# A hybrid decoder layer on one core: another order for the first loads, and the 16 meta rows' statistics on another engine

## The chip, the cores and the metric

The kernel runs on one core of a Trainium2 chip. The metric is the device time of one execution in microseconds. Five engines work side by side, each with its own instruction queue: TensorE (PE, with its weight loads shown as PEld), VectorE (DVE), ScalarE (ACT), GpSimd (POOL) and SyncE (SP), which here issues nearly all loads and stores.

## The reference

One decoder layer on 16 learned meta rows and 1024 rows of `x`, each 1024 wide, all in 32-bit floats. Everything begins with a normalisation of each row and one wide projection:

```python
def rmsnorm(x, g):
    xf = x.astype(jnp.float32)
    y = xf * lax.rsqrt(jnp.mean(xf * xf, axis=-1, keepdims=True) + EPS)
    return (y * g.astype(jnp.float32)).astype(x.dtype)

h = jnp.concatenate([meta, x], axis=1)          # 16 + 1024 rows
a = rmsnorm(h, ln_mix_pre[l])
proj = a @ w_in[l]                              # 1024 -> 3584 columns
dq, dk, dv, hq, hf, hi, hg = jnp.split(proj, SPLITS, axis=-1)
y_diff = diff_attention(dq, dk, dv, ...)        # 4 heads
y_hgrn = hgrn2(hq, hf, hi, hg, ...)             # 4 heads, a gated recurrence
mix = jnp.concatenate([y_diff, y_hgrn], axis=-1) @ w_out[l]
h = h + rmsnorm(mix, ln_mix_post[l])
a = rmsnorm(h, ln_ffn_pre[l])
y = conv_ffn(a, ...)                            # 1024 -> 5632, conv of 3, gelu, 2816 -> 1024
h = h + rmsnorm(y, ln_ffn_post[l])
return h[:, N_META:, :]
```

The change touches only the first `rmsnorm`, for the first 272 rows.

## The kernel before

The rows are cut into nine blocks: block 0 holds the 16 meta rows, blocks 1 to 8 hold 128 rows of `x` each. The projection takes them in three groups of three blocks, so the first matmuls of the first group need blocks 0, 1 and 2. To keep the precision of 32-bit floats, each operand is split into a rounded part (`ahi`, `wh`) and the rest (`alo`, `wl`), and three products are summed.

For each block the first normalisation has these steps. `load_x` (L266) issues the load on SP, the meta rows' if the block is 0. `pre_stat` (L270) squares the rows on ScalarE with a running sum; then `rstd_of` (L169) turns the sum into the reciprocal root with two small ScalarE instructions, Ln and Exp. `pre_scale` (L278) multiplies one half (512 columns) by the root and by the gain, on VectorE. `pre_turn` (L283) transposes four squares of 128 columns on TensorE into one bank of its accumulator memory. `pre_hi` (L291) casts that into `ahi` on ScalarE, and `pre_lo` (L294) writes the rest into `alo` on VectorE.

The gain is one row of 1024 numbers, loaded into `grow` (L793). Two matmuls (L835) with a row of ones spread it over 128 partitions, 512 columns each, and VectorE copies each half into `gb`, which every `pre_scale` reads.

```python
def pre_stat(i):
    r = rows(i)
    xss[i] = zp.tile([P, D], F32, tag="xs", name=f"xs{i}", bufs=3)
    ss = zp.tile([P, 1], F32, tag="ss", name=f"ss{i}", bufs=3)
    A.activation(xss[i][:r], xts[i][:r], AF.Square, accum_out=ss[:r])
    rstd_of(ss[:r], ss[:r], D)
    return ss

def pre_scale(i, half, ss):
    r = rows(i)
    cs = slice(512 * half, 512 * half + 512)
    V.scalar_tensor_tensor(xss[i][:r, cs], xts[i][:r, cs], ss[:r], gb[:r, cs], ALU.mult, ALU.mult)
```

`weights(j, c)` (L821) splits half `c` of the weights of projection `j` (0 is `dq`, 1 is `dk`): the cast of `dq`'s weights is on ScalarE, that of `dk`'s on GpSimd, and the rest of both (`wl`) on GpSimd. The third, `dv`, follows later (`third_hi`, `third_lo`). Blocks 4 and 5 are scaled by `far_block` (L874): ScalarE multiplies by the root, GpSimd by the gain.

Order: TensorE runs in the order of the program throughout. From L828 (`state["ordered"] = True`) to L952 VectorE, ScalarE and GpSimd do so too; `V`, `A` and `G` are wrappers whose instructions all appear under L58 in the profile. After L952 a planner places the instructions of the engines other than TensorE by its own estimated times. SP issues the loads in the order in which they stand, each when its slot is free. `xt` tiles have three slots, which `grow`, block 0 and block 1 take first, and later blocks 6, 7 and 8; blocks 2 to 5 use spare memory (`X_in`). The transposes use a pool of five banks; the gain's two halves take two of them first, and the turned half (2, 1) takes the bank of (0, 0) again, so it waits for `pre_lo` of (0, 0).

Of the kernel before, what the change touches and what calls it, by code (L numbers as in the profile page):

```python
# [9 lines left out]
F32 = mybir.dt.float32  # L10
# [3 lines left out]
ALU = mybir.AluOpType  # L14
AX = mybir.AxisListType
PSUM = bass.MemoryType.PSUM

P = 128
# [3 lines left out]
D = 1024  # L22
# [19 lines left out]
def rows(i):  # L42
    return META if i == 0 else P
# [47 lines left out]
def layer_kernel(ctx: ExitStack, tc: tile.TileContext, x, meta, table, lbl, gpre, gpost, win,  # L91
# [3 lines left out]
    V, A = Ordered(tc, nc.vector, state), Ordered(tc, nc.scalar, state)  # L95
# [3 lines left out]
    def pool(name, bufs, side="left", space=None):  # L99
        kw = {"side": side} if space is None else {"space": space}  # L100
        cm = tc.tile_pool(name=name, bufs=bufs, reuse_waits="tile", **kw)
        return cm, cm.__enter__()
# [44 lines left out]
    def ps_m(name):  # L147
        return pp.tile([P, 512], F32, tag="m", name=name, bufs=deep["m"])
# [20 lines left out]
    def rstd_of(dst, ss, n):  # L169
        A.activation(dst, ss, AF.Ln, bias=eps[: dst.shape[0]], scale=1.0 / n)  # L170
        return A.activation(dst, dst, AF.Exp, scale=-0.5)
# [5 lines left out]
    def mix_tile(tag, dt, name):  # L177
        return mxp.tile([P, MIX[tag]], dt, tag=tag, name=name)
# [51 lines left out]
    z_cm, zp = pool("pre", 2, "right")  # L230
# [30 lines left out]
    xts, xss = {}, {}  # L261

    def spare_tile(tag):
        return mix_tile(tag, F32, f"{tag}_in")

    def load_x(i, where=None):  # L266
        xts[i] = zp.tile([P, D], F32, tag="xt", name=f"xt{i}", bufs=3) if where is None else where
        SY.dma_start(xts[i][: rows(i)], meta if i == 0 else x[P * (i - 1): P * i, :])
# [14 lines that stand above are left out]
    def pre_turn(i, half, pt):  # L283
        r = rows(i)
        for j in range(4):
            k = 4 * half + j
            T.transpose(pt[:, j * r:(j + 1) * r], xss[i][:r, P * k: P * (k + 1)], ident[:r, :r])
        pv = pt[:, : 4 * r].rearrange("p (k t) -> p k t", k=4)
        return pv, slice(4 * half, 4 * half + 4), slice(place(start(i)), place(start(i)) + r)

    def pre_hi(pv, ks, s):  # L291
        return A.copy(ahi[:, ks, s], pv)
# [325 lines left out]
    def attn_in(h):  # L618
        qs = [ap_.tile([P, L], F32R, tag=f"q{m}", name=f"q{m}_{h}") for m in range(2)]
        ks = [ap_.tile([P, L], F32R, tag=f"k{m}", name=f"k{m}_{h}") for m in range(2)]  # L620
        vn = ap_.tile([P, NBLK, P], F32, tag="avn", name=f"avn{h}")
        G.memset(vn[:, 0], 0.0)
        rr = ap_.tile([P, 256], F32, tag="rr", name=f"rr{h}")
        own = [slice(0, 64), slice(64, 128)]
        oth = [slice(64, 128), slice(0, 64)]

        def ev_q(g, b0, b1, t0, t1, pt):
            for m in range(2):
                A.mul(qs[m][own[m], t0:t1], pt[own[m]], 0.125)
            for m in range(2):  # L630
                V.scalar_tensor_tensor(qs[m][oth[m], t0:t1], pt[own[m]], 0.125, qs[m][own[m], t0:t1].bitcast(F32), ALU.mult, ALU.subtract)

        def ev_k(g, b0, b1, t0, t1, pt):
            for m in range(2):
                A.copy(ks[m][own[m], t0:t1], pt[own[m]])
            for m in range(2):
                V.tensor_tensor(kl[m][own[m], t0:t1], pt[own[m]], ks[m][own[m], t0:t1].bitcast(F32), op=ALU.subtract)
            for m in range(2):
                A.copy(ks[m][oth[m], t0:t1], ks[m][own[m], t0:t1].bitcast(F32))

        def ev_v(g, b0, b1, t0, t1, pt):
            vt = ap_.tile([P, 384], F32, tag="vt", name=f"vt{h}_{g}", bufs=1)
            A.copy(vt[:, : t1 - t0], pt)
            late.append((vn, vt, b0, b1, f"va{h}_{g}"))

        return (qs, ks, vn, rr), [(h, f"dq{h}", ev_q), (4 + h, f"dk{h}", ev_k), (8 + h, f"dv{h}", ev_v)]
# [144 lines left out]

    t_a, tiles = attn_in(0)
    grow = zp.tile([P, D], F32, tag="xt", name="grow", bufs=3)[:1]  # L793
    SY.dma_start(grow, gpre)
    spare = {n: spare_tile(t) for n, t in ((2, "X0"), (0, "X1"), (1, "X2"))}
    load_x(0)
    load_x(1)
    load_x(2, spare[2][:, :D])

    def raw_tile(j, c):  # L800
# [20 lines left out]
    def weights(j, c):  # L821
        hi = wp.tile([P, 512], F32R, tag="wh", name=f"wh_{tiles[j][1]}_{c}", bufs=4)
        lo = wp.tile([P, 512], F32R, tag="wl", name=f"wl_{tiles[j][1]}_{c}", bufs=4)
        (G.tensor_copy if j else A.copy)(hi, raws[j, c])
        G.tensor_tensor(lo, raws[j, c], hi.bitcast(F32), op=ALU.subtract)
        parts[j][c] = hi, lo

    state["ordered"] = True  # L828
    stat = {}
    for i in range(3):  # L830
        stat[i] = pre_stat(i)
    for half in range(2):
        cs = slice(512 * half, 512 * half + 512)
        pt = ps_m(f"pg{half}")
        T.matmul(pt, ones, grow[:, cs], start=True, stop=True)  # L835
        V.tensor_copy(gb[:, cs], pt)
        if half == 0:
            pre_scale(0, 0, stat[0])
    load_x(6)
    banks0 = {}  # L840
    for i in range(3):
# [1 line left out]
    turned = {}  # L843

    def turn(i, half):
        turned[i, half] = pre_turn(i, half, banks0[i][half])

    for i in (1, 2):
        for half in range(2):
            pre_scale(i, half, stat[i])  # L850
    pre_scale(0, 1, stat[0])
    for i, half in ((0, 0), (1, 0), (1, 1), (2, 0), (2, 1), (0, 1)):
        turn(i, half)
    pre_hi(*turned[0, 0])
    pre_hi(*turned[1, 0])
    weights(0, 0)
    pre_hi(*turned[2, 0])
    for i in range(3):
# [900 lines left out]
```

## Time and profile before

| | |
|---|---|
| three runs | 1276.09, 1278.28, 1279.64 us, median 1278.28 |
| the profiled execution | 1277.19 us, its span 1275.4 us |
| TensorE busy | 1256.7 us, 99% of the span |
| VectorE, ScalarE, GpSimd busy | 913.9, 687.3, 507.2 us |
| granted TensorE clock | 0.999 |

A row of the timeline has the start and the duration in microseconds, the engine, the line, the operation, what is written and read, and in brackets how long the engine had been idle before and what released it. `x4` behind a row means that neighbouring like instructions were merged. In a table by stretches, each row has the stretch, its length, the busy time of PE, PEld, DVE, ACT and POOL, the granted clock, the busy share of the DMA engines and the GB/s that they moved.

### The profile page before, as it was taken

What the parts mean: (1) busy time and instruction counts of PE and PEld (TensorE: products, weight loads), DVE (VectorE), ACT (ScalarE), POOL (GpSimd) and SP (SyncE); (2) the same over time, 40 slices, a digit from 0 to 9 for tenths busy, and PEclk for the clock granted to TensorE, in tenths of its full rate; (3) what the DMA queues carried; (4) which work ended last, traced back from release to release, by engine and by line L of the source; (5) the groups of instructions that cost most, each with busy time, mean ns of one, the idle gap of its engine ahead of it and who ended that gap; (6) DMA issues with size and microseconds to landing.
All of it is one profiled execution on the core that took longest, in us unless ns stands there. A gap on an engine that the chain in (4) does not pass through costs nothing.

```text
span 1275.4 us, 26064 instructions
## 1 busy us (share of the span) xinstructions
PE 1256.7 (99%) x10166; PEld 1172.8 (92%) x10166; DVE 913.9 (72%) x1492; ACT 687.3 (54%) x1638; POOL 507.2 (40%) x390
## 2 busy tenths in 40 slices
PE   8999999999999999999999999999999999999997
PEld 6999999999999998778899999999999998878886
DVE  7565646565656564457899888898898877797586
ACT  8475456546654754356764544445535445564554
POOL 5232423241323311353067676676776731020121
PEclk9999999999999999999999999999999999999999
DMA  7336555373734533787322221322222247955363
GB/s 260 96 60 131 89 139 94 83 146 92 132 94 79 125 82 113 232 279 253 131 67 67 92 88 63 100 76 75 92 75 83 75 116 258 351 184 173 91 215 124
DMA packets 116705, 165.04 MB, mean 129 GB/s; under 512 B 10131, under 2 KB 57811, under 8 KB 116582
## 3 DMA queue, kind: packets, MB, share of 16 engines
q1 hardware_dynamic: 93350, 151.84, 37.1%
q0 software_dynamic: 23232, 11.54, 7.7%
q8 instruction: 80, 1.31, 0.4%
q14 instruction: 43, 0.35, 0.1%
HBM read 134.24 MB, written 52.17 MB: 146 GB/s over the span
## 4 chain that ended last, share of the span: by engine, by line
PE 46%; DVE 4%; ACT 2%; issue 1%; POOL 1%; DMA 0%; SPq 0%; DVEq 0%; ACTq 0%; POOLq 0%
PE pd L1586 5%; PE pd L1587 5%; PE pd L1585 5%; PE pb L1412 4%; PE pb L1411 4%; PE pb L1413 4%; PE pc L1412 3%; PE pc L1411 3%; PE pc L1413 3%; PE pa L1412 3%; PE pa L1411 3%; PE pa L1413 3%; DVE xh L58 1%; DVE t L58 1%; DVE c L58 1%
## 5 line engine op out<-in xcount | busy, mean ns | idle before, releaser
L1412 PE MATMUL pb<-t,uh 128*128 128x258 f32 x504 | 141.0, 280 | 0.8 <-DVE t L58 0.8
L1411 PE MATMUL pb<-t,uh 128*128 128x258 f32 x504 | 140.5, 279 | 0.8 <-DVE u L58 0.8
L1413 PE MATMUL pb<-t,ul 128*128 128x258 f32 x504 | 140.2, 278 | 0.0
L1586 PE MATMUL pd<-wl,gh 128*128 128x512 f32 (+1 forms) x312 | 121.0, 388 | 1.1 <-DVE wl L58 1.1
L1585 PE MATMUL pd<-wh,gh 128*128 128x512 f32 (+1 forms) x312 | 120.8, 387 | 0.5 <-DVE x L58 0.5
L1587 PE MATMUL pd<-wh,gl 128*128 128x512 f32 (+1 forms) x312 | 120.7, 387 | 0.0
L58 DVE SCALAR_TENSOR_TENSOR c<-uu,cwt,c 128x514 f32<-128x514 f32 (+1 forms) x88 | 106.9, 1214 | 0.0
L58 DVE SCALAR_TENSOR_TENSOR c<-ug,cwt,c 128x514 f32<-128x514 f32 (+1 forms) x88 | 101.4, 1153 | 0.0
L1412 PEld LDWEIGHTS pb<-t,uh 128*128 128x128 f32 x504 | 94.8, 188 | 1.0 <-DVE t L58 1.0
L1411 PEld LDWEIGHTS pb<-t,uh 128*128 128x128 f32 x504 | 94.8, 188 | 1.0 <-DVE u L58 1.0
L58 ACT ACTIVATE c<-c 128x514 f32<-128x514 f32 (+1 forms) x44 | 27.9, 634 | 125.5 <-DVE c L58 125.5
L1413 PEld LDWEIGHTS pb<-t,ul 128*128 128x128 f32 x504 | 94.8, 188 | 0.0
L1412 PE MATMUL pc<-t,uh 128*128 128x258 f32 (+1 forms) x336 | 93.9, 279 | 0.0
L1412 PE MATMUL pa<-t,uh 128*128 128x258 f32 (+1 forms) x336 | 93.9, 279 | 0.0
L1411 PE MATMUL pa<-t,uh 128*128 128x258 f32 (+1 forms) x336 | 93.6, 278 | 0.0
L1411 PE MATMUL pc<-t,uh 128*128 128x258 f32 (+1 forms) x336 | 93.6, 278 | 0.0
L1413 PE MATMUL pc<-t,ul 128*128 128x258 f32 (+1 forms) x336 | 93.4, 278 | 0.0
L1413 PE MATMUL pa<-t,ul 128*128 128x258 f32 (+1 forms) x336 | 93.4, 278 | 0.0
L58 POOL TENSOR_TENSOR ul<-ws,uh 128x512 fp32r<-128x512 f32 x42 | 69.2, 1647 | 59.6 <-ACT uh L58 59.6
L58 POOL TENSOR_TENSOR ws<-ra,ra 128x512 f32<-128x512 f32 x42 | 67.9, 1617 | 60.9 <-DMA ra<-in_wup_dram 34.1
L58 POOL TENSOR_TENSOR c<-c,c 128x514 f32<-128x514 f32 (+1 forms) x44 | 68.8, 1564 | 53.9 <-ACT c L58 50.5
L58 DVE TENSOR_TENSOR ul<-ra,uh 128x512 fp32r<-128x512 f32 x43 | 41.5, 966 | 46.6 <-POOL ul L58 46.6
(389 smaller groups left out, 4183.1 us busy)
## 6 DMA issues: line engine op xcount, KB each, us to landing
ra<-in_wup_dram SPq DMA_DIRECT2D x88, 256.0 KB, 2.6
mp<-msc SPq DMA_DIRECT2D x23, 512.0 KB, 5.7
tsc<-in_wdown_dram SPq DMA_DIRECT2D x44, 256.0 KB, 5.2
wi<-tsc SPq DMA_DIRECT2D x44, 256.0 KB, 3.0
gi<-gsc SPq DMA_DIRECT2D x33, 256.0 KB, 4.2
wi<-in_wdown_dram SPq DMA_DIRECT2D x33, 256.0 KB, 5.2
gsc<-c SPq DMA_DIRECT2D x22, 257.0 KB, 2.1
tsc<-in_wdown_dram POOLq DMA_DIRECT2D x22, 256.0 KB, 7.2
```

What stands on the lines that cost most here:

```text
L58: ins = call(*args, **kw)
L1411: T.matmul(pt, hi[:, s], th[:, k], start=(first and k == 0), stop=False, skip_group_check=True)
L1412: T.matmul(pt, hi[:, s], tl[:, k], start=False, stop=False, skip_group_check=True)
L1413: T.matmul(pt, lo[:, s], th[:, k], start=False, stop=(k == 3), skip_group_check=True)
L1585: T.matmul(py, gh[:, s], wh, start=(k == 0 and pr not in (3, 7)), stop=False, skip_group_check=True)
L1586: T.matmul(py, gh[:, s], wl, start=False, stop=False, skip_group_check=True)
L1587: T.matmul(py, gl[:, s], wh, start=False, stop=(k == NH - 1), skip_group_check=True)
```

## The change

SP issues the load of block 1 first, then the meta rows, then `grow`; before it was `grow`, the meta rows, block 1. The meta rows' squares and their sum move from one ScalarE instruction to two VectorE instructions ahead of the gain's copies; the reciprocal root of the meta rows stays on ScalarE, now between the statistics of blocks 1 and 2. The first half of the meta rows is scaled behind both halves of block 1, where it was scaled between the gain's two copies. Its transposes go behind those of block 1, and its cast `pre_hi` behind that of (1, 0).

```diff
     t_a, tiles = attn_in(0)
     grow = zp.tile([P, D], F32, tag="xt", name="grow", bufs=3)[:1]
+    spare = {n: spare_tile(t) for n, t in ((2, "X0"), (0, "X1"), (1, "X2"))}
+    load_x(1)
+    load_x(0)
     SY.dma_start(grow, gpre)
-    spare = {n: spare_tile(t) for n, t in ((2, "X0"), (0, "X1"), (1, "X2"))}
-    load_x(0)
-    load_x(1)
     load_x(2, spare[2][:, :D])
...
     state["ordered"] = True
     stat = {}
-    for i in range(3):
-        stat[i] = pre_stat(i)
+    r = rows(0)
+    xss[0] = zp.tile([P, D], F32, tag="xs", name="xs0", bufs=3)
+    stat[0] = zp.tile([P, 1], F32, tag="ss", name="ss0", bufs=3)
+    V.tensor_tensor(xss[0][:r], xts[0][:r], xts[0][:r], op=ALU.mult)
+    V.reduce_sum(stat[0][:r], xss[0][:r], axis=AX.X)
+    stat[1] = pre_stat(1)
+    rstd_of(stat[0][:r], stat[0][:r], D)
+    stat[2] = pre_stat(2)
     for half in range(2):
         cs = slice(512 * half, 512 * half + 512)
         pt = ps_m(f"pg{half}")
         T.matmul(pt, ones, grow[:, cs], start=True, stop=True)
         V.tensor_copy(gb[:, cs], pt)
-        if half == 0:
-            pre_scale(0, 0, stat[0])
     load_x(6)
...
-    for i in (1, 2):
-        for half in range(2):
-            pre_scale(i, half, stat[i])
+    for half in range(2):
+        pre_scale(1, half, stat[1])
+    pre_scale(0, 0, stat[0])
+    for half in range(2):
+        pre_scale(2, half, stat[2])
     pre_scale(0, 1, stat[0])
-    for i, half in ((0, 0), (1, 0), (1, 1), (2, 0), (2, 1), (0, 1)):
+    for i, half in ((1, 0), (1, 1), (0, 0), (2, 0), (2, 1), (0, 1)):
         turn(i, half)
+    pre_hi(*turned[1, 0])
     pre_hi(*turned[0, 0])
-    pre_hi(*turned[1, 0])
     weights(0, 0)
     pre_hi(*turned[2, 0])
     for i in range(3):
         pre_lo(*turned[i, 0])
```

## The prediction

> **What bounds the kernel now.** I read the page first, then the busy time by stretches, because a change in the first microseconds is worth only what the stages behind it let through.
>
> ```profile
> span 1275.4 us, 26064 instructions
> PE 1256.7 (99%) x10166; PEld 1172.8 (92%) x10166; DVE 913.9 (72%) x1492; ACT 687.3 (54%) x1638; POOL 507.2 (40%) x390
> ```
> ```profile
> 0.00:26.00 26.00, 20.76 (x122) 16.73 (x123) 18.08 (x27) 21.15 (x46) 18.11 (x27) 1.00 0.79 282
> 26.00:60.00 34.00, 33.80 (x201) 31.07 (x200) 20.59 (x48) 18.85 (x45) 7.44 (x11) 1.00 0.34 105
> 60.00:200.00 140.00, 139.90 (x1355) 135.70 (x1356) 82.73 (x193) 83.59 (x250) 43.21 (x40) 1.00 0.52 108
> ...
> 400.00:600.00 200.00, 197.67 (x1583) 173.18 (x1582) 116.75 (x215) 109.65 (x325) 64.73 (x53) 1.00 0.57 169
> 600.00:800.00 200.00, 197.54 (x1630) 193.84 (x1629) 175.00 (x214) 111.12 (x215) 115.03 (x72) 1.00 0.28 91
> ```
>
> The second column of a stretch is its length, the third TensorE's busy time. TensorE is idle 5.2 us of the first 26 and only 0.3 of the next 174. So a delay or a gain that reaches TensorE's queue at 26 us goes through to the end; nothing behind it is slack that could swallow it. The question is what sets TensorE's pace in the first 26 us. I followed that through the timeline, engine by engine.
>
> ```profile
> 0.73 0.35 SPq L794 DMA_DIRECT2D grow<-in_gpre_dram  x1
> 1.14 0.33 SPq L268 DMA_DIRECT2D xt<-in_meta_dram  x1
> 1.52 0.41 SPq L268 DMA_DIRECT2D xt<-in_x_dram  x1
> 1.97 0.43 SPq L268 DMA_DIRECT2D X_in<-in_x_dram  x1
> ```
> ```profile
> 2.30 3.75 PE L835 MATMUL pg<-grow,ones 1*128 1x512 f32 x4 [2.30 <-DMA grow<-in_gpre_dram]
> 4.38 0.69 DVE L58 COPY gb<-pg 128x512 f32<-128x512 f32 x1 [4.38 <-PE pg L835]
> 6.08 0.69 DVE L58 COPY gb<-pg 128x512 f32<-128x512 f32 x1 [0.17 <-PE pg L835]
> 7.02 1.42 DVE L58 SCALAR_TENSOR_TENSOR xs<-xt,ss,gb 128x512 f32<-128x512 f32 x2 [0.24 <-ACT ss L58]
> ```
> ```profile
> 5.28 1.06 ACT L58 ACTIVATE xs<-xt 128x1024 f32<-128x1024 f32 x1 [0.37 <-DMA xt<-in_x_dram]
> 6.78 0.20 ACT L58 ACTIVATE ss<-ss 128x1 f32<-128x1 f32 x1
> 6.89 1.04 ACT L58 ACTIVATE xs<-X_in 128x1024 f32<-128x1024 f32 x1
> ```
>
> Columns are start, duration, engine, operation, and in brackets the idle time before it and its releaser. The scaling of block 1 (7.02) needs two things: the reciprocal root of block 1, ready at 6.78 + 0.20 = 6.98, and the gain row spread over the partitions, whose second half is copied by 6.08 + 0.69 = 6.77. The gain chain begins with the small load `grow`, and it is **only 0.2 us** ahead of the chain that the change wants to shorten. That is the centre of my argument.
>
> ```profile
> 7.83 3.18 PEld L287 LDWEIGHTS px<-ident,xs 128*128 128x128 f32 x16 [1.29 <-DVE xs L58]
> 6.06 0.58 PE L287 MATMUL px<-ident,xs 16*128 16x16 f32 x4
> 8.98 0.59 ACT L58 CAST ahi<-px 128x512 fp32r<-128x512 f32 x1 [0.29 <-PE px L287]
> 9.46 0.62 ACT L58 CAST wh_dq<-wr_dq 128x512 fp32r<-128x512 f32 x1
> 10.69 1.07 ACT L58 CAST ahi<-px 128x512 fp32r<-128x512 f32 x2 [0.60 <-PE px L287]
> 10.17 1.66 POOL L58 TENSOR_TENSOR wl_dq<-wr_dq,wh_dq 128x512 fp32r<-128x512 f32 x1 [6.17 <-ACT wh_dq L58]
> 14.96 1.07 POOL L58 CAST wh_dk<-X_in 128x512 fp32r<-128x512 f32 x1
> 21.27 2.53 POOL L58 TENSOR_TENSOR xs<-xs,gb 128x512 f32<-128x512 f32 x2 [0.88 <-ACT xs L58]
> 25.09 0.55 PEld L901 LDWEIGHTS pi_dv<-ahi,w 128*128 128x128 f32 x4 [0.81 <-POOL w L58]
> ```
>
> From 10.17 on GpSimd works with one gap of 0.88 us, and TensorE's last wait in the head, at 25.09, is for GpSimd. What starts GpSimd is the cast `wh_dq` on ScalarE at 9.46, queued there behind `pre_hi` of blocks 0 and 1. So the head's end is set by when that cast starts.
>
> **The change part by part.** Times are this trace's; the moved ones are worked out.
>
> *Block 1's load first.* It is issued at 0.73 in place of 1.52.
>
> ```profile
> xt<-in_x_dram SPq DMA_DIRECT2D x1, 512.0 KB, 3.7
> xt<-in_meta_dram SPq DMA_DIRECT2D x1, 64.0 KB, 2.0
> sub<-in_subln_dram SPq DMA_DIRECT2D x1, 0.5 KB, 7.8
> 4.00:4.50 0.50, 0.50 (x2) 0.33 (x1) 0.12 (x1) 0.40 (x3) 0.00 (x0) 1.00 0.96 393
> ```
>
> With the 3.7 us that it takes now (the last column: issue to landing) it lands at 4.43; its square and statistics take 5.28 to 6.98, that is 1.70, so its root is ready at 6.15, 0.8 earlier. The block of 512 KB after these three keeps its place.
>
> *`grow` third.* Issued at 0.73 + 0.45 + 0.38 = 1.56, the steps being those of the block and the meta rows now. When does it land? At the head of the queue it takes about 2.27 − 0.73 = 1.54 us; alone, it would land at 3.1. But `sub`, only 0.5 KB, takes 7.8 us when it is issued behind full blocks: a small load on this queue waits for the bytes ahead of it. By that row `grow` comes behind 512 and 64 KB, and the meta rows behind 512. At 393 GB/s (last column) 64 KB are 0.16 us, so meta and `grow` land at about 4.6. An upper end is 5.22, where the third load of the same 580 KB landed before (1.52 + 3.7). I take 4.6, nearest to the `sub` row, and keep 3.1 and 5.2 as ends. `grow` is **2.3 us later**.
>
> The Trainium skill, "DMA: Bandwidth & Descriptors", under "Queues, rings and completion order", says that each DMA engine takes the descriptors of one ring in order, which speaks against this move and agrees with the 7.8 us. Its fit under "Anatomy of one DMA" (about 2.0 us and the bytes over 436 GB/s, given for another queue kind) would have `grow` at 1.56 + 2.0 = 3.6 if nothing stood ahead; by that alone the end would come 1.0 us earlier than I forecast.
>
> *The gain chain.* From TensorE's start at 2.30 to the second copy at 6.08 it takes 3.78 us, so from 4.6 the second copy runs 8.4 to 9.1, and scaling of block 1 starts at 9.1 in place of 7.02: **+2.1**. The 0.8 that block 1 won ends in a wait.
>
> *Meta squares and sum on VectorE.* Two instructions on 16x1024, which the trace does not show; nearest are
>
> ```profile
> L58 DVE TENSOR_TENSOR t<-at,t 128x1024 fp32r<-128x1024 f32 x8 | 9.6, 1217 | 0.1
> L58 DVE TENSOR_REDUCE ast<-S 128x1 f32<-128x912 f32 x8 | 8.9, 1107 | 0.2
> 5.17 0.74 DVE L58 SCALAR_TENSOR_TENSOR xs<-xt,ss,gb 16x512 f32<-16x512 f32 x1
> ```
>
> The 16-row scaling of 512 costs as much as the 128-row one (0.74 against 1.42/2), so rows don't matter: 1.22 + 1.11 × 1024/912 = 2.5 us. From 4.6 that ends at 7.1. First gain copy 7.1 to 7.8, then a wait to 8.4: the work is hidden by TensorE's second gain matmul, with 0.6 to spare; if `grow` were early that cover would be gone, and the second copy would run 7.8 to 8.5. ScalarE sheds a 1.06 square but now waits from 6.15 to 7.1 in `rstd_of` for the sum, and block 2's square stands behind that: 7.6 in place of 6.89. Block 2's root then comes at about 9.3, needed only at 11. Free.
>
> *Order of scaling, turning and casts.* VectorE's scalings follow each other by about 0.7: (1,0) 9.1, (1,1) 9.8, (0,0) 10.4, (2,0) 11.1, (2,1) 11.8, (0,1) 12.5. TensorE turns four squares in about 0.85 (3.18 for sixteen loads, plus the drain), starting 0.8 after the scaling starts: (1,0) from 9.9, (1,1) 10.75, then (0,0) 11.6 to 12.2 (0.58 now). `pre_hi` of (0,0) has become the second cast and must wait for that: 12.3. Then `wh_dq` at 12.4 or 12.5 in place of 9.46. Of these 3.0 us, 2.1 are the gain chain and 0.9 the new place of (0,0), which now stands behind two turned halves of block 1 instead of ahead of them. This 0.9 has nothing to do with the load and stays even if `grow` is early.
>
> *Behind it.* GpSimd's chain starts 3.0 later and drags the `dk` weights, block 3's turn and the last wait at 25.09. ScalarE's own chain is 2.5 to 2.9 later (cast of (2,0) at about 13.3 in place of 10.69), so the gap of 0.88 may give back up to 0.3. I take **+2.9** at 26 us, and as ends +1.5 (0.6 + 0.9, if meta and `grow` both overtake) and +3.6 (`grow` at 5.2).
>
> *Slots.* `xt` has three slots, first held by `grow`, block 1 and the meta rows and then by blocks 6, 7 and 8. Block 8's load now waits for the meta rows' last scaling, at 13.2.
>
> ```profile
> xt<-in_x_dram SPq DMA_DIRECT2D x1, 512.0 KB, 8.5
> 29.40 1.05 ACT L58 ACTIVATE xs<-xt 128x1024 f32<-128x1024 f32 x1
> L58 ACT CAST wh_hf<-wr_hf x2: 620/621/622, 45.7 to 48.2; 128x512 fp32r<-128x512 f32 x2
> ```
>
> Even with 8.5 us it lands at 21.7 and is read at 29.4 or later; the small loads and the `hf` weights queued behind it on SP are used at 45.7. Nothing.
>
> **Sum.** The profiled execution took 1277.19 us, so + 2.9 is 1280.1 on its base; it lies 1.1 below the median of the runs, 1278.28. On the median the forecast is 1278.28 + 2.9 = **1281.2**. About 0.3% (3.8 us) is what a measurement can tell from no change, so this is a loss on the near side of that: over 1282.1 would be slower.
>
> **The rivals.** *The small loads overtake.* If meta (1.18 + 2.0 = 3.2) and `grow` (3.1) take only their own times, the sum ends at 5.7, the second gain copy at 7.6, scaling starts 0.6 late, and with the 0.9 the head loses 1.5: 1279.8. For it: the DMA engines still move little just then (66 GB/s, last column). Against it: the `sub` row.
>
> ```profile
> 2.50:3.00 0.50, 0.50 (x1) 0.26 (x2) 0.00 (x0) 0.00 (x0) 0.45 (x2) 1.00 0.58 66
> ```
>
> *A new order later gives it back (the other side).* From line 952 on, the instructions of all engines but TensorE are placed by a planner from its own due times, which the change shifts. Place: the stretches 400 to 800 us, where TensorE now idles 2.3 + 2.5 = 4.8 us. If all of that went, 1281.2 − 4.8 = 1276.4; it decides the sign once it gives back over 2.9. For it: only that these stalls exist. Against: everything behind 26 us shifts together, and then an order by due times stays.
>
> *A new order later costs a further stall.* The same mechanism the other way, one stall as large as one of these two stretches holds now: 1281.2 + 2.4 = 1283.6. A stage filled to 99.9% has more to lose than to win, so I hold it likelier than the gain.
>
> That the change does what it says, and block 1's turns start sooner, can't pay: even with `grow` where it was, the gain chain's 6.77 allows 0.2 us at (1,0), which the new place of (0,0) takes back.
>
> **How the numbers follow.** Forecast 0.48 (own range 1280.4 to 1282.3), overtaking 0.12, an order that gives back 0.08, an order that costs 0.32. The giving back lies 2 us above the border of 1274.4; half of its chance, and 0.01 for what I don't see, is faster: 0.05. Slower over 1282.1 is most of the costing order and the forecast's upper edge: 0.35. The rest, 0.60, is within 0.3%. The range runs from the giving order's upper part, 1278.6, over the overtaking case to 1284.5, a costing order with the head at its upper end.
>
> **What would show it.** In the changed profile: SP issues block 1, meta, `grow` at 0.7, 1.2 and 1.6; the gain matmul starts near 4.6 (near 3.1: overtaking); scaling of block 1 at 9.1 with its wait put to TensorE's `pg`, not to ScalarE's root; `wh_dq` at 12.4; GpSimd's first weight operation near 13.2; the `pi_dv` weight load of 25.09 near 28; TensorE's busy time in the first 26 us down by about 2.9. I am wrong if the gain matmul starts before 3 us, if `wh_dq` starts before 10.5, or if the stretches 400 to 800 us lose or win over 2 us of TensorE's idle time.

## The result, and the profile after

The changed kernel takes 1280.21 us (median of 19 runs, 1277.43 to 1284.62) against 1277.01 of the kernel before (19 runs, 1274.67 to 1279.64) on the same chip: 3.2 us more. The ratio of the runs is 1.0029, its 95% interval 1.0020 to 1.0037, so the loss is about 2.6 to 4.7 us: clear of no change, and on both sides of the 0.3% border (3.8 us) that I had set. The ratio counts fast runs alone and need not be that of the medians, which is 1.0025 here. The profiled execution took 1279.47 us.

The page of the changed kernel, and its busy time by stretches (length, then TensorE, PEld, VectorE, ScalarE, GpSimd):

```profile
span 1277.7 us, 26064 instructions
PE 1257.1 (98%) x10166; PEld 1174.2 (92%) x10166; DVE 916.3 (72%) x1494; ACT 686.1 (54%) x1636; POOL 507.2 (40%) x390
```
```profile
0.00:26.00 26.00, 19.31 (x108) 15.78 (x109) 17.39 (x24) 18.02 (x39) 14.47 (x25) 1.00 0.82 279
26.00:60.00 34.00, 32.74 (x191) 29.57 (x190) 21.95 (x51) 20.46 (x49) 9.20 (x10) 1.00 0.24 79
60.00:200.00 140.00, 139.90 (x1358) 135.89 (x1357) 81.48 (x189) 80.87 (x242) 43.71 (x42) 1.00 0.50 110
400.00:600.00 200.00, 198.47 (x1620) 174.73 (x1620) 117.71 (x218) 111.24 (x328) 64.82 (x53) 1.00 0.57 168
600.00:800.00 200.00, 197.50 (x1617) 193.43 (x1617) 174.29 (x214) 110.68 (x213) 114.35 (x72) 1.00 0.27 93
```

TensorE idles 6.7 us in the first 26 (5.2 before) and 1.3 in the next 34 (0.2 before): 2.5 more in the head. Its last wait there is over 3.24 us later (below), so 0.7 of the delay does not show as idle time; as an estimate, TensorE is counted busy for that much longer because it runs slowly until 16.7 us here and until 10.7 before (see the same kernels once more). From 60 to 200 us TensorE's busy time has not changed. The head itself, from the timeline of the changed kernel:

```profile
0.73 0.39 SPq L268 DMA_DIRECT2D xt<-in_x_dram  x1
1.18 0.42 SPq L268 DMA_DIRECT2D xt<-in_meta_dram  x1
1.64 0.32 SPq L797 DMA_DIRECT2D grow<-in_gpre_dram  x1
```
```profile
4.51 1.06 ACT L58 ACTIVATE xs<-xt 128x1024 f32<-128x1024 f32 x1 [2.50 <-DMA xt<-in_x_dram]
4.83 1.21 DVE L58 TENSOR_TENSOR xs<-xt 16x1024 f32<-16x1024 f32 x1 [4.83 <-DMA xt<-in_meta_dram]
5.03 3.75 PE L841 MATMUL pg<-grow,ones 1*128 1x512 f32 x4 [5.03 <-DMA grow<-in_gpre_dram]
6.07 1.21 DVE L58 TENSOR_REDUCE ss<-xs 16x1 f32<-16x1024 f32 x1
8.81 0.69 DVE L58 COPY gb<-pg 128x512 f32<-128x512 f32 x1 [0.94 <-PE pg L841]
9.42 2.05 DVE L58 SCALAR_TENSOR_TENSOR xs<-xt,ss,gb 128x512 f32<-128x512 f32 x3
12.93 0.62 ACT L58 CAST wh_dq<-wr_dq 128x512 fp32r<-128x512 f32 x1
13.63 1.27 POOL L58 TENSOR_TENSOR wl_dq<-wr_dq,wh_dq 128x512 fp32r<-128x512 f32 x1 [9.63 <-ACT wh_dq L58]
13.86 1.07 ACT L58 CAST ahi<-px 128x512 fp32r<-128x512 f32 x2 [0.31 <-PE px L287]
24.52 2.53 POOL L58 TENSOR_TENSOR xs<-xs,gb 128x512 f32<-128x512 f32 x2 [1.05 <-ACT xs L58]
28.33 0.55 PEld L907 LDWEIGHTS pi_dv<-ahi,w 128*128 128x128 f32 x4 [0.81 <-POOL w L58]
```

Block 1 is there 0.77 us earlier (4.51 against 5.28), but the gain's matmul starts 2.73 later (5.03 against 2.30), and scaling has no idle time of its own at 9.42: it follows the second gain copy at once.

| step, start in us | before | forecast | after |
|---|---|---|---|
| block 1's square | 5.28 | 4.4 | 4.51 |
| meta rows there | 3.13 | 4.6 | 4.83 |
| the gain's matmul | 2.30 | 4.6 | 5.03 |
| second gain copy | 6.08 | 8.4 | 8.81 |
| scaling of block 1 | 7.02 | 9.1 | 9.42 |
| first cast of the `dq` weights | 9.46 | 12.4 | 12.93 |
| cast of block 2's first half | 10.69 | 13.3 | 13.86 |
| TensorE goes on after its last wait in the head | 25.09 | 28 | 28.33 |

The instruction lists of the two kernels, laid side by side engine by engine, differ in nothing behind the head: GpSimd's is the same throughout, and the others differ only in the instructions that the change moved or replaced.

### The profile page after: what moved, and what is told of

It reads as the page before. It is cut to its first block, busy times and chain, and to the rows that moved or that the text cites. A ratio compares the mean times of both kernels' runs of the same rounds, so it can differ in the third digit from the quotient of the medians.

```text
span 1277.7 us, 26064 instructions
## 1 busy us (share of the span) xinstructions
PE 1257.1 (98%) x10166; PEld 1174.2 (92%) x10166; DVE 916.3 (72%) x1494; ACT 686.1 (54%) x1636; POOL 507.2 (40%) x390
## 3 DMA queue, kind: packets, MB, share of 16 engines
q0 software_dynamic: 23232, 11.54, 7.7%
## 4 chain that ended last, share of the span: by engine, by line
PE 87%; DVE 4%; DMA 3%; ACT 2%; issue 1%; POOL 1%; SPq 0%; DVEq 0%; ACTq 0%; POOLq 0%
PE pd L1592 5%; PE pd L1593 5%; PE pd L1591 5%; PE pb L1418 4%; PE pb L1417 4%; PE pb L1419 4%; PE pa L746 3%; PE pa L1418 3%; PE pc L1418 3%; PE pc L1417 3%; PE pa L1417 3%; PE pc L1419 3%; PE pa L1419 3%; PE pt L722 2%; PE S L666 1%; PE S L665 1%
```

## The experiments

The reading that I took into them (theory A): 2.4 of the loss at the `dq` cast come from the gain row's place in the queue and the rest from the meta rows' new place in the order. Against it: that VectorE's two new instructions delay (B), and that the DMA engines, not the queue, make the small loads late (C). Each kernel is read at the same points of its own profile; the last two columns compare its runs with the runs of the kernel before beside it (9 to 12 against 20 to 30, for the changed kernel 19 against 19). The median is a difference in us. I go by the ratio and its interval.

| kernel | gain matmul | block 1 scaled | `dq` cast | last wait over | median | ratio, interval |
|---|---|---|---|---|---|---|
| before | 2.30 | 7.02 | 9.46 | 25.09 | | |
| changed | 5.03 | 9.42 | 12.93 | 28.33 | +3.2 | 1.0029, 1.0020 to 1.0037 |
| loads alone | 5.35 | 9.74 | 12.18 | 28.32 | +3.5 | 1.0025, 1.0014 to 1.0036 |
| computing alone | 2.24 | 7.08 | 10.60 | 27.15 | +1.4 | 1.0010, 1.0001 to 1.0019 |
| gain row first | 2.55 | 9.11 | 12.61 | 29.12 | +3.8 | 1.0026, 1.0017 to 1.0035 |
| other queue | 2.78 | 9.63 | 13.13 | 29.46 | +5.0 | 1.0031, 1.0020 to 1.0041 |
| cast first | 5.35 | 9.74 | 12.24 | 29.97 | +3.6 | 1.0029, 1.0017 to 1.0040 |
| computing, TensorE busy | 2.40 | 7.03 | 10.50 | 25.75 | +1.0 | 1.0004, 0.9996 to 1.0013 |
| changed, TensorE busy | 5.08 | 9.51 | 12.95 | 28.21 | +4.8 | 1.0031, 1.0022 to 1.0041 |
| before, TensorE busy | 2.37 | 6.94 | 9.65 | 25.80 | +0.7 | 1.0000, 0.9991 to 1.0009 |

**The loads alone.** The kernel before, with

```diff
-    SY.dma_start(grow, gpre)
     spare = {n: spare_tile(t) for n, t in ((2, "X0"), (0, "X1"), (1, "X2"))}
-    load_x(0)
     load_x(1)
+    load_x(0)
+    SY.dma_start(grow, gpre)
```

> The kernel before with the changed load order alone (block 1, meta rows, gain row); all computing as before. Theory A (the delay is the gain row's place in the load queue plus the meta rows' new place in the order): the gain matmul starts at 5.0 as in the changed kernel, the second gain copy ends at 9.5, block 1 is scaled from 9.5 (before 7.02, changed 9.42), the first cast of the dq weights starts at 11.9 to 12.0 (before 9.46, changed 12.93), TensorE's last wait for GpSimd in the head ends at 27.4 to 27.7 (before 25.09, changed 28.33); time +2.4 us on before. Theory B (the two VectorE instructions for the meta rows are what delays): all of this stays within 0.5 of before.

The gain's matmul, the scaling and the cast came where theory A put them, 0.2 to 0.3 later. The last wait is over at 28.32, 0.6 later than expected and as late as in the whole change. Behind the cast of block 2's first half (13.40) the head takes 14.9 us here, and 14.4 from that cast (10.69) in the kernel before. This 0.5 is VectorE, on whose scaling the transposes of block 3 wait: it takes 2.88 us here for the two halves of block 3, 1.93 in the kernel before and 1.82 in the changed kernel. The loads alone, then the changed kernel:

```profile
17.37 2.88 DVE L58 SCALAR_TENSOR_TENSOR xs<-X_in,ss,gb 128x512 f32<-128x512 f32 x2
```
```profile
17.82 1.82 DVE L58 SCALAR_TENSOR_TENSOR xs<-X_in,ss,gb 128x512 f32<-128x512 f32 x2
```

So the order of the loads by itself makes the loss, without VectorE's new instructions, and B falls as the only cause. About 2.7 of its 3.2 us in the head are the late gain row, and 0.5 the slower scaling.

**The computing alone.** The changed kernel, with the loads in the order of before (the same three lines the other way).

> The changed kernel with the load order of before (gain row, meta rows, block 1). Theory A: gain matmul at 2.3, VectorE's square and sum 3.1 to 5.6, gain copies done by 7.0, block 1 scaled from 7.0 to 7.1, the meta rows' first half is turned behind two halves of block 1, so the first cast of the dq weights starts at 10.4 to 10.5, the last wait for GpSimd ends at 25.7 to 26.1; time +0.8 us on before, inside what can be told. Theory B: block 1 scaled from 9 or later, time +2.5 us or more.

Scaling starts at 7.08: with the meta rows there at 3.1, VectorE's square and sum are free. The `dq` cast starts 1.1 later than before, which is the new place of (0,0) that I had put at 0.9. But the last wait is over at 27.15, not at 26: 2.06 later than before, nearly twice the delay of the cast. Something else was at work there, and this is what the experiments from the cast first on are about.

**The gain row first.** The changed kernel with

```diff
+    SY.dma_start(grow, gpre)
     load_x(1)
     load_x(0)
-    SY.dma_start(grow, gpre)
```

> The changed kernel with the gain row's load first, then block 1, then the meta rows. If the gain row's place alone mattered: block 1 scaled from 7.0, dq cast at 10.5, last wait for GpSimd at about 26, time +0.9 us. My expectation is another: the meta rows land at about 5.2 behind block 1, their square and sum on VectorE run to 7.6 and the gain copies, queued behind them, to 9.0, since TensorE's second gain matmul, which covered them, is long over. Then block 1 is scaled from 9.0, the dq cast starts at 12.5 and the last wait ends at 27.8; time +2.7 us, nearly as slow as the changed kernel although the gain row is there 2.7 us earlier.

```profile
2.55 3.75 PE L841 MATMUL pg<-grow,ones 1*128 1x512 f32 x4 [2.55 <-POOL kl L58]
5.53 1.22 DVE L58 TENSOR_TENSOR xs<-xt 16x1024 f32<-16x1024 f32 x1 [5.53 <-DMA xt<-in_meta_dram]
6.78 1.21 DVE L58 TENSOR_REDUCE ss<-xs 16x1 f32<-16x1024 f32 x1
7.92 1.27 DVE L58 COPY gb<-pg 128x512 f32<-128x512 f32 x2
9.11 2.06 DVE L58 SCALAR_TENSOR_TENSOR xs<-xt,ss,gb 128x512 f32<-128x512 f32 x3
```

With the gain's matmul 2.5 us earlier than in the changed kernel, block 1 is scaled only 0.3 earlier. The first gain matmul could be copied from 4.6 on, but the copies stand behind the meta rows' sum, and the meta rows now wait behind block 1. The cover that the prediction named, TensorE's gain matmul, is gone and the 2.4 us of VectorE work lie on the path. The two causes don't add; each hides behind the other. The last wait is over at 29.12, 1.3 later than I expected: as in the computing-alone kernel, ScalarE waits 1.24 us for the transposes of block 3.

**The small loads on another queue.** The changed kernel, with `grow` and then the meta rows issued from ScalarE's queue:

```diff
...
     load_x(1)
-    load_x(0)
-    SY.dma_start(grow, gpre)
+    nc.scalar.dma_start(grow, gpre)
+    load_x(0, queue=nc.scalar)
```

> The changed kernel with the gain row's and the meta rows' loads issued from ScalarE's own queue, block 1 first on SP's. If the small loads wait because of their place in SP's queue (theory A): the gain matmul starts by 2.4 to 3.6 though block 1 is being loaded, meta lands by 4.2, block 1 lands at 4.5, the gain copies are done by 7.3, block 1 scaled from 7.0 to 7.4, dq cast 10.4 to 10.9, last wait 25.9 to 26.4, time +1 us on before. If they wait because the DMA engines themselves are full with block 1, whatever the queue (theory C): the gain matmul starts at 4.5 or later, and everything is as in the changed kernel, +3 us.

```profile
0.76 0.51 ACTq L796 DMA_DIRECT2D grow<-in_gpre_dram  x1
1.29 0.34 ACTq L268 DMA_DIRECT2D xt<-in_meta_dram  x1
2.78 3.75 PE L841 MATMUL pg<-grow,ones 1*128 1x512 f32 x4 [2.78 <-DMA grow<-in_gpre_dram]
6.05 1.21 DVE L58 TENSOR_TENSOR xs<-xt 16x1024 f32<-16x1024 f32 x1 [6.05 <-DMA xt<-in_meta_dram]
```

Half of theory A came out. The gain row takes 2.0 us beside block 1's load, not 3.4: for it, the queue was the cause. But the 64 KB of the meta rows took 4.7 us, and came later than behind block 1 in SP's own queue (4.83 in the changed kernel). A queue of their own gave them no right of way over blocks 1 and 2 and the weights, which SP's queue was loading by then. Why the one load got through and the other not, these runs don't tell. The outcome is that of the gain row first: VectorE's work uncovered, scaling at 9.63, and ScalarE waiting 1.06 for block 3.

**The cast first.** The changed kernel with

```diff
     pre_hi(*turned[1, 0])
-    pre_hi(*turned[0, 0])
     weights(0, 0)
+    pre_hi(*turned[0, 0])
```

> The changed kernel with the first cast of the dq weights put ahead of the meta rows' cast, so that it no longer waits for their transposes. If the head's end is set by when GpSimd starts (the prediction's reading): the cast starts at 11.9 in place of 12.93, GpSimd starts about 1.0 earlier and the last wait ends at 27.3 to 27.5 in place of 28.33; time 0.9 us less than the changed kernel. If ScalarE's own chain sets it (from the cast of block 2's first half, at 13.86, it is busy without a gap until block 5 is scaled, and GpSimd waits for that): GpSimd starts 1.0 earlier, its gap ahead of block 5 grows from 1.05 to about 2, and the last wait stays at 28.1 to 28.4; time as the changed kernel.

```profile
12.94 1.32 POOL L58 TENSOR_TENSOR wl_dq<-wr_dq,wh_dq 128x512 fp32r<-128x512 f32 x1 [8.94 <-ACT wh_dq L58]
22.22 1.07 ACT L58 CAST ahi<-px 128x512 fp32r<-128x512 f32 x2 [1.45 <-PE px L287]
26.16 2.52 POOL L58 TENSOR_TENSOR xs<-xs,gb 128x512 f32<-128x512 f32 x2 [2.76 <-ACT xs L58]
29.97 0.55 PEld L907 LDWEIGHTS pi_dv<-ahi,w 128*128 128x128 f32 x4 [0.81 <-POOL w L58]
```

GpSimd starts 0.69 earlier and its gap ahead of block 5 grows from 1.05 to 2.76, so the start of GpSimd does not set the end of the head: this reading of the prediction falls. But the end is 1.6 later than in the changed kernel, which neither theory had; 0.3 of it is the gain row, which landed that much later in this profile. ScalarE, which in the changed kernel is busy without a gap here, waits 1.45 for TensorE's transposes of block 3.

**The same kernels once more.** What differs is TensorE's own pace, which its loads of weights show. The kernel before and the computing-alone kernel were profiled a second time:

> The kernel before, unchanged, profiled a second time. In its first profile four transposes take 0.85 us from 7.8 to 10.6 and the matmuls from 11.2 on run at twice that rate; in the changed kernel the change of rate comes at 16.7, in the kernel with its computing alone also at 16.7, and with the gain row first at 18.7. If the moment is a matter of chance in each execution, it moves here by over 1 us, and with it the end of the last wait in the head (25.09). If the kernel's own pattern of work sets it: 10.4 to 10.9 again, last wait at 25.0 to 25.2.

> The kernel with the changed computing and the loads of before, unchanged, profiled a second time. By chance: the rate changes at another time than 16.7, and the last wait ends between 26.0 (early) and 27.5 instead of at 27.15. By the kernel's own pattern: 16.4 to 17.0 and 27.0 to 27.3 again.

The kernel before, first and second profile:

```profile
11.52 0.56 PEld L901 LDWEIGHTS pi_dq<-ahi,wh_dq 128*128 128x128 f32 x4
```
```profile
11.95 0.95 PEld L901 LDWEIGHTS pi_dq<-ahi,wh_dq 128*128 128x128 f32 x4
12.80 0.71 PEld L901 LDWEIGHTS pi_dk<-ahi,wh_dk 128*128 128x128 f32 x4
13.45 0.56 PEld L901 LDWEIGHTS pi_dq<-ahi,wl_dq 128*128 128x128 f32 x4
25.04 0.55 PEld L901 LDWEIGHTS pi_dv<-ahi,w 128*128 128x128 f32 x4 [0.81 <-POOL w L58]
```

Computing alone, first profile:

```profile
15.48 1.01 PEld L907 LDWEIGHTS pi_dq<-alo,wh_dq 128*128 128x128 f32 x4
16.39 0.82 PEld L907 LDWEIGHTS pi_dk<-alo,wh_dk 128*128 128x128 f32 x4
17.15 0.56 PEld L907 LDWEIGHTS pi_dk<-ahi,wl_dk 128*128 128x128 f32 x4
19.39 1.08 ACT L58 CAST ahi<-px 128x512 fp32r<-128x512 f32 x2 [1.26 <-PE px L287]
```

Four weight loads take 0.95 to 1.01 us until some moment and 0.56 after it. In the kernel before, the moment was 10.5 to 10.9 in one profile and 13 in the other, so it moves between executions; the last wait did not (25.09 and 25.04), since these matmuls have slack there. In the computing-alone kernel it was between 16.7 and 16.9 in both, and there it costs: ScalarE waits 1.26 (1.19 in the second profile) for block 3. I call the slow stretch half rate and what follows full rate.

**TensorE kept busy.** Four matmuls of the identity by itself, overwritten by the transposes, in the idle time of the computing-alone kernel; it was profiled twice.

```diff
     turned = {}
+    for _ in range(4):
+        T.matmul(banks0[1][0][:, :P], ident, ident, start=True, stop=True)
```

> The kernel with the changed computing and the loads of before, with four more matmuls of the identity by itself, whose result is overwritten, on TensorE between the gain's matmuls and the first transposes, where it idled from 6.0 to 8.0. If what costs the last 0.9 us in the head of that kernel is that TensorE runs at half rate until 16.7, and idling is why: full rate comes by 13, four dq or dk matmuls take 0.5 instead of 0.9 us, block 3 is transposed by 17.7 in place of 18.6, ScalarE waits less than 0.4 for it, and the last wait ends at 26.1 to 26.4; time 0.9 us less than without them. If the rate isn't what delays, or more work doesn't bring it: 27.0 to 27.3, or later by what the four cost (up to 0.2).

> The kernel with the changed computing, the loads of before and four more matmuls in TensorE's idle time, profiled a second time. In its first profile TensorE is at full rate by 11 and the last wait of the head ends at 25.75; without the four, two profiles have 16.7 and 16.8, and 27.15 and 27.14. If the four matmuls set the rate: full rate by 10.5 to 11.5 again, last wait at 25.6 to 25.9. If it was chance: full rate later than 12, and beyond 16 the last wait is back at 27.0 or later.

```profile
11.02 1.08 ACT L58 CAST ahi<-px 128x512 fp32r<-128x512 f32 x2
11.66 0.55 PEld L909 LDWEIGHTS pi_dq<-ahi,wh_dq 128*128 128x128 f32 x4
17.97 1.07 ACT L58 CAST ahi<-px 128x512 fp32r<-128x512 f32 x2 [0.37 <-PE px L287]
25.75 0.55 PEld L909 LDWEIGHTS pi_dv<-ahi,w 128*128 128x128 f32 x4 [0.82 <-POOL w L58]
```

In the kernel without the four matmuls, first profile, the same cast of block 2's first half is

```profile
11.54 1.07 ACT L58 CAST ahi<-px 128x512 fp32r<-128x512 f32 x2 [0.31 <-PE px L287]
```

The second profile has full rate before 9.8 and its last wait over at 25.45. So in this kernel TensorE's half rate costs 1.4 to 1.7 us at the end of the head (27.15 and 27.14 against 25.75 and 25.45). It is paid in two places: 0.5 and 1.0 in the transposes ahead of that cast (11.54 and 11.60 against 11.02 and 10.62), the rest in ScalarE's wait for block 3. I had expected only the second, hence 26.1 to 26.4. The ends 25.75 and 25.45 are 0.4 to 0.7 later than those of the kernel before; that is not the price of the computing part by itself, since the transposes of the kernel before ran at half rate, and no profile shows it at full rate ahead of them. The gain is one of the head; in the time, 1.0004 against 1.0010, the intervals overlap.

The same in the other two kernels: seven such matmuls ahead of the gain's and three behind in the changed kernel, three behind the first transposes in the kernel before.

> The changed kernel with TensorE kept busy in its idle time: seven matmuls of the identity ahead of the gain's matmuls (it waits there for the gain row until 5.0) and three behind them, all overwritten. If idling is why TensorE runs at half rate: full rate by 7, the gain's matmuls take 2 to 3 instead of 3.75, the second gain copy is then bound by VectorE's meta work (8.0 to 8.6 in place of 9.5 at its end), block 1 scaled from 8.5, transposes in half the time, the first cast of the dq weights at 11.2 to 11.8 (12.93), the last wait ends at 26.4 to 27.0 (28.33); time 1.5 to 2 us less than the changed kernel, still 1 to 1.5 us over before. If the rate is not what idling sets: 28.2 or later, no gain.

```profile
1.58 3.06 PEld L842 LDWEIGHTS pg<-ident 128*128 128x128 f32 x14 [1.58 <-POOL ident masks.py:199]
5.08 3.78 PE L843 MATMUL pg<-grow,ones 1*128 1x512 f32 x4
12.20 1.84 PEld L287 LDWEIGHTS px<-ident,xs 16*128 16x128 f32 x12 [0.33 <-issue]
28.21 0.55 PEld L911 LDWEIGHTS pi_dv<-ahi,w 128*128 128x128 f32 x4 [0.81 <-POOL w L58]
```

> The kernel before with three matmuls of the identity in TensorE's idle time from 6.6 to 7.8, overwritten. If full rate comes earlier by it: transposes at full rate from 9 to 10, block 2's first half cast at 10.0 to 10.5 in place of 10.69, the last wait ends at 24.4 to 24.9 in place of 25.04 to 25.09; time 0.2 to 0.6 us less, too little to be told from before. If not: 25.0 to 25.2 and the time of before.

Both fell short of what I expected. In the changed kernel TensorE has work from 1.58 with few gaps, and yet the gain's matmuls take 3.78 and full rate comes only at about 14; the last wait is over 0.1 earlier. In the kernel before, full rate came at 12, between the two moments seen without the three, and the last wait was over at 25.80, 0.7 later: 0.2 at the cast of block 2's first half (10.88), the rest behind it. There VectorE took 2.88 us for the two halves of block 3, as with the loads alone, where the kernel before takes 1.93, while GpSimd's cast beside it fell from 1.07 to 0.61. So filling idle time doesn't bring full rate early by itself, and that the four matmuls did it in the computing-alone kernel rests on two profiles against two.

**The changed kernel once more.**

> The changed kernel, unchanged, profiled a second time. Its first profile has TensorE at half rate until 16.7 and the last wait ending at 28.33; the variant with the cast first had half rate until 19.9 and 29.97. If the moment is chance and the changed kernel exposed to it: half rate until somewhere between 14 and 20, and the last wait ends later the later it is, up to 29.9; up to 16.7 it stays at 28.2 to 28.4. If it is fixed: 16.4 to 17.0 and 28.2 to 28.5.

```profile
16.97 0.64 PEld L907 LDWEIGHTS pi_dq<-ahi,wl_dq 128*128 128x128 f32 x4
20.78 1.08 ACT L58 CAST ahi<-px 128x512 fp32r<-128x512 f32 x2 [0.25 <-PE px L287]
28.53 0.55 PEld L907 LDWEIGHTS pi_dv<-ahi,w 128*128 128x128 f32 x4 [0.81 <-POOL w L58]
```

Full rate at 17.1 instead of 16.7, and the last wait over 0.2 later, of which 0.07 is the gain row, there at 5.10. The variant with ten more matmuls, at full rate from about 14, had its last wait over at 28.21. Against it, what was still at half rate behind the transposes cost the changed kernel 0.1 in its first profile and 0.3 in the second. All its transposes ran at half rate in both; what full rate ahead of them would be worth was not seen. No kernel among these beats the kernel before; its variant with the three matmuls has its time.

## Why the prediction was right or wrong

**The time and its sign** were right: +2.9 forecast, +3.2 measured between the medians (3.7 by the ratio), and +2.3 between the spans of the two profiled executions. That the number fits so well is in part luck: the head lost 3.24, and 0.9 of that came back behind it in these two executions, which the forecast did not have. One sign of the prediction failed: TensorE's busy time in the first 26 us fell by 1.45, not by 2.9, since the delay reaches past 26 us and TensorE was at half rate for longer.

**The gain row in the queue** was right in kind and 0.4 short: it came at 5.03, with my upper end at 5.2. The loads-alone kernel shows that this term makes the loss without any other part, and the other-queue kernel that the 4 KB do not wait when they stand in another queue. Overtaking, the rival, did not happen in SP's queue in any run.

The Trainium skill, "DMA: Bandwidth & Descriptors", under "Queues, rings and completion order", has each DMA engine take the descriptors of one ring in order; the gain row's 3.4 us behind block 1 and 2.0 us in another queue agree with it. The fit of "Anatomy of one DMA", by which it would have been there at 3.6, did not hold behind other loads. For a gain row at 3.6 the prediction has the end 1.0 us earlier; by its own sum it is 0.6, since the second gain copy would then run from 7.8 to 8.5 behind VectorE's work, and scaling would start at 8.5 in place of 9.1.

**VectorE's work hidden, free only as long as `grow` is late** was right: 0.94 us of cover were left, where I had 0.6, and with the gain row first it was on the path. 1.21 and 1.21 were measured for 1.22 and 1.24 worked out.

**0.9 for the place of (0,0)** measured 1.1, in the computing-alone kernel and in the changed one alike.

**"The head's end is set by when that cast starts" was wrong.** In the changed kernel GpSimd has a gap of 1.05 behind its first eight instructions, where it waits for ScalarE, and it gave back 0.4 already in its first (1.27 in place of 1.66). The end follows ScalarE's chain from the cast of block 2's first half: 3.17 later (13.86 against 10.69), and the last wait 3.24 later. I had that chain at +2.5 to 2.9, and only as what gives a little back. The forecast came out because both chains start from the same transposes, which is luck as far as this step goes. The cast-first kernel takes them apart.

**What the prediction did not have at all** is TensorE's half rate. It had read the 0.85 us of four transposes as their cost, and they are that only at half rate; at full rate four take 0.42 to 0.48. For its sum this did no harm, since the transposes of both kernels ran at half rate. What came behind them cost the changed kernel 0.1 to 0.3; in the computing-alone kernel the half rate made up to 1.7 of the head.

**The two rivals of a new order** fell on the instruction lists. In the place where I put them, 400 to 800 us, TensorE idles 4.8 and 4.4 us in the two profiles of before and 4.0 and 3.4 in those of the changed kernel; nearly all of the difference is in 400 to 600 (2.33 and 2.43 against 1.53 and 1.44). That may be why the spans differ by less than the heads. The order of the instructions there is the same, and among the other kernels the idle time of 400 to 600 runs from 0.6 to 3.4, so I can't say what it comes from, and it wasn't tried.

## What to carry to other kernels

Before a large load is put ahead of small ones on one queue, ask what chain starts from the small ones: 0.8 us won for a block cost 2.7 us on a 4 KB row that a matmul chain of 3.8 us hangs on. When two chains end within 0.2 us of each other, shortening one is worth that 0.2 us, and work that is moved under the cover of the other must be priced again for the case that this cover goes. The gain row's place and VectorE's new work are such a pair: put back alone, the gain row won 0.3 us at the scaling. An experiment that undoes one part of a change can lose as much as the whole, so read it at several points of the profile and not only by its time.

## What the runs showed of the hardware

TensorE ran its first matmuls at about half its later rate in every profile, until some moment between 9 and 20 us, while the granted clock in the rows by stretches stood at 1.00. It is seen in the duration of like instructions: 0.95 to 1.01 us against 0.56 for four weight loads. The Trainium skill, "TensorE: Matmul & The Clock Gate", in its Part 1, describes such a half rate, which ends after about 3.4 us of sustained work as seen by a free-running window. The moment's move from 10.7 to 13 in two profiles of one kernel agrees with that; the changed kernel with ten more matmuls, at work from 1.58 with few gaps and at half rate until about 14, does not. Whether that is chance or hangs on the kind of work, these runs don't show.

On a queue of their own, 64 KB took 4.7 us from issue to landing beside the 1 MB of blocks 1 and 2, and weights behind them, that SP's queue was loading, longer than behind half of it in the same queue (3.6 in the changed kernel). The 4 KB ahead of them took 2.0 us from issue to use.

VectorE's two scalings of block 3 (128x512 each) took 1.80 to 2.88 us beside GpSimd, where two such scalings took 1.42 in the kernel before while GpSimd was idle (7.02). In the two profiles with 2.88 (the loads alone, and the kernel before with TensorE busy) GpSimd's cast started within 0.04 us of them and took 0.62 and 0.61; in the kernel before and the changed kernel it started 0.2 to 0.3 us after them and took 1.07 and 1.08. No run was made to find out what decides between the two; it moved the end of the head by about 0.5 us.
